# Four half tiles each on GpSimd, an adding DMA and a casting DMA: another way to split gate weights in a hybrid trunk layer

## The chip, the cores and the metric

The kernel runs on one core of one Trainium2 chip. The metric is the device time of one execution in microseconds, from runs without a profile. Beside it stands one profiled execution, whose span runs from its first to its last instruction.

## What is computed

One layer of a decoder trunk, for 256 positions of width 2048 in fp32. Cut to what matters here:

```python
h = rms_norm(x, pre_g)
a_u, a_v, a_g, b_x, b_g, x_q, x_g, gate_logits = split(h @ w_in)
y_a = spatial_gating(a_u, a_v, ...) * silu(a_g)
y_b = s5_branch(b_x, ...) * silu(b_g)
y_x = memory_cross_attention(x_q, rms_norm(mem, mem_g), wk, wv) * silu(x_g)
branch = einsum('bsnc,ncd->bsnd', stack([y_a, y_b, y_x]), w_branch)
gates = sigmoid(gate_logits)                  # 3 branches x 2048 columns
merged = sum(gates * branch, over the branches)
out = x + rms_norm(merged @ w_out, post_g)
```

The change touches the weights of `gate_logits` for one of the three branches, the cross-attention (n = 2): a matrix of 2048 x 2048.

## The kernel before, in words

**Splitting.** TensorE multiplies in the float32r format, which keeps fewer bits than fp32. So every fp32 operand is split in two: a high part, which is the operand rounded to float32r, and a low part, the operand minus the high part, rounded too. A product is made of three matmuls: high by high, high by low and low by high (`tm_mm`, L180 to L182). The split of weights stands in `split_to`: ScalarE copies the raw tile into the high part (L92), VectorE subtracts (L93).

**Tiles of weights.** `load` (L78, on SP's queue) brings a raw tile of 128 x 2048 fp32 (1 MB) from HBM; there are three such buffers (`rawp`). Each raw tile is split in two halves of 1024 columns, the half tiles. A half tile's high and low part lie in one tile called `hl`, of which there are four (`hip`, `bufs=4`). `split` makes one and marks the two instructions as early ones: `tc.high_priority(offset=AHEAD)`, with `AHEAD = 250`, moves them 250 places forward in the order in which the planner takes up instructions.

**Order.** TensorE's instructions are issued in the order in which the program writes them (`manual_schedule`). The order on the other engines is made by a planner that lays out the instructions by priority and by estimated durations when the program is built. Each engine then works through its own list in order and waits where an input isn't there or a buffer isn't free.

**Token-major products.** `tm_quarter` (L218 to L225) takes one raw tile: for each of its halves it calls `split`, then issues twelve matmuls of 512 columns (two blocks of 128 rows of weights, two blocks of 128 positions, three matmuls each), then calls `pump`. `merge(n, ...)` (L771 to L784) runs over four column blocks c of 512 columns. For each it makes the gate logits from four raw tiles (eight half tiles), takes the sigmoid (L781), makes the branch's own product from two raw tiles (four half tiles) and hands both to a sink, which multiplies them on VectorE (L791).

**Background work.** The S5 branch runs as a generator beside all this. `pump` lets it go on by a credit after each half tile; `rate["tm"]` sets the credit, and for n = 2 it is 0.33 higher in the first column block and 0.13 higher in the second. Its work is mostly VectorE's (products L371, scans L599, L374 for updates), with some on ScalarE (L530, L534, L535, L540, L548, L555) and a few matmuls (L560, L624). GpSimd issues its loads, one of 128 KB for each of 32 steps (L518, tile `sb`), and hardly anything else: one masking instruction (L814) after this merge.

**Where the merges stand.** `merge(2, ...)` is the first of the merges. In the profiled execution its column blocks c = 1, 2 and 3 run on TensorE from 265.27, 298.22 and 330.95 us of the span.

Of the kernel before, what the change touches and what calls it, by code (L numbers as in the profile page):

```python
# [9 lines left out]
F32 = mybir.dt.float32  # L10
# [3 lines left out]
AF = mybir.ActivationFunctionType  # L14
ALU = mybir.AluOpType
# [28 lines left out]
def trunk(ctx: ExitStack, tc: tile.TileContext, I, out):  # L44
    nc = tc.nc
    v, a, g, pe = nc.vector, nc.scalar, nc.gpsimd, nc.tensor
# [18 lines left out]
    def nm(s):  # L65
        n_[0] += 1
        return f"{s}_{n_[0]}"

    def slot(tag, shape, dt=F32):
        return big.tile(shape, dt, tag=tag, name=nm(tag))  # L70
# [5 lines left out]
    def load(src):  # L76
        t = rawp.tile([P, 2048], F32, tag="raw", name=nm("raw"))
        nc.sync.dma_start(out=t, in_=src)  # L78
        return t

    def halves(off):
        t = hip.tile([P, 2 * 1024 + 128], F32R, tag="hl", name=nm("hl"))
        return t[:, off:off + 1024], t[:, off + 1024:off + 2048]

    def split(src, off=0):
        hi, lo = halves(off)
        with tc.high_priority(offset=AHEAD):
            split_to(hi, lo, src)
        return hi, lo

    def split_to(hi, lo, src):
        a.copy(out=hi, in_=src)  # L92
        v.tensor_tensor(out=lo, in0=src, in1=hi.bitcast(F32), op=ALU.subtract)  # L93
# [16 lines left out]
    def acc_tile():  # L110
        return accp.tile([P, 2, 512], F32, tag="acc", name=nm("acc"))
# [67 lines left out]
    def tm_mm(ps, wh, wl, hl, tb, first, last):  # L179
        pe.matmul(ps, lhsT=hl.stationary(0, tb), rhs=two(wh), start=first, stop=False)  # L180
        pe.matmul(ps, lhsT=hl.stationary(0, tb), rhs=two(wl), start=False, stop=False)  # L181
        pe.matmul(ps, lhsT=hl.stationary(1, tb), rhs=two(wh), start=False, stop=last)  # L182
# [3 lines left out]
    def pump(credit):  # L186
        with tc.high_priority(offset=-BEHIND):
            pump_(credit)
# [21 lines left out]
    def cm_block(ps, raw, hl, mm_=cm_mm):  # L210
        for hf in range(2):
            wh, wl = split(raw[:, hf * 1024:(hf + 1) * 1024], CM_OFF)
            for k in range(8):
                kk = hf * 8 + k
                mm_(ps, wh[:, k * P:(k + 1) * P], wl[:, k * P:(k + 1) * P], hl[kk], kk == 0, kk == 15)
            pump(rate["cm"])

    def tm_quarter(acc, raw, hl, kq, nk):  # L218
        for hf in range(2):
            wh, wl = split(raw[:, hf * 1024:(hf + 1) * 1024])  # L220
            for k in range(2):
                kk = kq * 4 + hf * 2 + k
                sl = slice(k * 512, (k + 1) * 512)
                for tb in range(2):
                    tm_mm(acc[tb], wh[:, sl], wl[:, sl], hl[kk], tb, kk == 0, kk == nk - 1)  # L225
            pump(rate["tm"])
# [20 lines left out]
    xhl = [Pairs(xp.tile([P, 2, 2, P], F32R, name=f"x{k}")) for k in range(16)]  # L247
    u = slot("U", [P, 8, T])
    acc0 = [acc_tile(), acc_tile()]
    for pc in range(8):  # L250
        if pc == 0:
            raw = first
        elif pc < 3:
            raw = rawp.tile([P, 2, 768], F32, tag="raw", name=nm("st"), padded_shape=[P, 2, 1024])
        else:
            raw = slot(("H0", "H1", "H2", "H3", "M0")[pc - 3], [P, 2, 1024])[:, :, 0:768]
        wh, wl = (z.rearrange("p (q n) -> p q n", q=2) for z in halves(CM_OFF))
# [421 lines left out]
    def tm_rows(src, hl, dst, key):  # L679
        for n in range(2):  # L680
            acc = acc_tile()
            for kq in range(4):
                tm_quarter([acc[:, 0], acc[:, 1]], load(src[n, kq]), hl, kq, 16)
            for tb in range(2):
                a.activation(out=dst[:, tb, n * 512:(n + 1) * 512], in_=acc[:, tb], func=AF.Copy,
                             scale=nrm[key][0][:, tb:tb + 1])
# [84 lines left out]
    def merge(n, yhl, sink):  # L771
        for c in range(4):
            rate["tm"] = RT[6] + (0.33, 0.13, 0.0, 0.0)[c] * (n == 2)
            G = acc_tile()
            for kq in range(4):
                tm_quarter([G[:, 0], G[:, 1]], load(I["w_gate"][n, c, kq]), xhl, kq, 16)
            assert not bg[2]
            Bp = acc_tile()
            sg = wk.tile([P, 2, 512], F32, tag="w0", name=nm("g"))
            for tb in range(2):  # L780
                a.activation(out=sg[:, tb], in_=G[:, tb], func=AF.Sigmoid, scale=rstd_x[:, tb:tb + 1])  # L781
            for kq in range(2):
                tm_quarter([Bp[:, 0], Bp[:, 1]], load(I["w_br"][n, c, kq]), yhl, kq, 8)
            sink(c, sg, Bp)  # L784
# [20 lines left out]

    mg = Lazy()
    merge(2, hls(yX), sink_first)

    vt = slot("H0", [P, 2, W])
# [73 lines left out]

    cm_pairs(I["w_au"], 8, xhl, evac_au)
    merge(0, hls(yA), sink_mid)
    nrm["A"] = True

# [4 lines left out]
    for c in range(4):  # L892
        G = acc_tile()
# [10 lines left out]
    for bp in range(4):  # L904
        ps = acc_tile()
        raw = load(I["glu"][bp])
        for b in range(2):
            wh, wl = split(raw[:, b * 1024:(b + 1) * 1024], CM_OFF)
            for k in range(8):
                cm_mm(ps[:, b], wh[:, k * P:(k + 1) * P], wl[:, k * P:(k + 1) * P], ygl[k], k == 0, k == 7)  # L910
        t = fold(ps, None)
        for i in range(2):
            a.activation(out=t[:, i, :], in_=t[:, i, :], func=AF.Sigmoid, bias=glu_b[:, 2 * bp + i:2 * bp + i + 1])
        b = slice(2 * bp, 2 * bp + 2)
        v.tensor_tensor(out=t, in0=t, in1=u[:, b, :], op=ALU.mult)
        v.tensor_tensor(out=t, in0=t, in1=sb[:, b, :], op=ALU.mult)
        for i in range(2):
            d = yB[2 * bp + i]
            split_to(d[:, 0], d[:, 1], t[:, i])
# [51 lines left out]
    for n in range(3):  # L971
        acc = acc_tile()
        for kq in range(4):
            tm_quarter([acc[:, 0], acc[:, 1]], load(I["w_out"][n, kq]), mhl2, kq, 16)
            if (n * 4 + kq) in (1, 4, 7):
                dst, src = late.pop(0)
# [7 lines left out]
    acc = acc_tile()  # L984
    for kh in range(2):
        raw = load(I["w_out3"][0, kh])
        for hf in range(2):
            wh, wl = split(raw[:, hf * 1024:(hf + 1) * 1024])
# [12 lines left out]
    for kh in range(2):  # L1001
        raw = load(I["w_out3"][1, kh])
        for hf in range(2):
            src = raw[:, hf * 1024:(hf + 1) * 1024]
            if kh == 0 and hf == 0:
                for i in range(2):
                    wh = s5p.tile([P, 512], F32R, tag="s", name=nm("wh"), bufs=4)
                    wl = s5p.tile([P, 512], F32R, tag="s", name=nm("wl"), bufs=4)
                    split_to(wh, wl, src[:, i * 512:(i + 1) * 512])
                    wks += [(wh[:, k * T:(k + 1) * T], wl[:, k * T:(k + 1) * T]) for k in range(2)]  # L1010
            else:
                wh, wl = split(src)
# [5 lines left out]
    for tb in range(2):  # L1018
# [3 lines left out]
        c = slice(tb, tb + 1)  # L1022
# [107 lines left out]
```

## Time and profile before

| | |
|---|---|
| time, median of two runs | 917.31 us (917.14 to 917.48) |
| profiled execution: span | 915.4 us |
| TensorE (PE) busy | 902.2 us, 99% |
| VectorE (DVE) busy | 779.5 us, 85% |
| ScalarE (ACT) busy | 535.0 us, 58% |
| GpSimd (POOL) busy | 22.2 us, 2% |
| HBM read | 190.39 MB, 210 GB/s over the span |

The time before is that of runs without a profile; the page names the span of the profiled execution and no other time of it.

How to read the lines: a line such as `L93 DVE TENSOR_TENSOR hl<-raw,hl 128x1024 ... x319 | 388.5, 1221 | 97.3 <-ACT hl L92 93.8` is a group: line of the program, engine, operation, output and inputs, shape, count; then busy time in us and mean ns of one; then the engine's idle time just before these instructions, and what ended most of it. In order of time, a line has the start and the duration in us, and in brackets the idle time ahead of it and what released it. PEld is the weight load of a matmul, which overlaps the matmuls. A matmul's duration is modelled and longer than the distance to the next one, so TensorE's progress is read from starts. POOLq, SPq and ACTq are the queues on which DMAs are issued.

### The profile page before, as it was taken

Reading aid. Unit: us, or ns where it says so; the run is one execution under the profiler, and the core shown is the slowest. Engines: PE = TensorE matmul, PEld = TensorE weight load, DVE = VectorE, ACT = ScalarE, POOL = GpSimd, SP = SyncE. Lnnn points to the kernel's source line nnn. Section 1 sums busy time; section 2 is a strip of 40 time slices with the busy share of each in tenths; the row PEclk is TensorE's granted clock in tenths of the full one; section 3 lists DMA queues with packets and bytes.
Section 4 is the critical chain, followed back from the end, with each engine's and each line's share of the span. In section 5 each row is a group of like instructions: output and inputs, shape, how many; then the busy total and the mean of one; then the engine's idle time right before and its main releaser. Section 6 shows DMA issues by size and latency. Waiting matters only on the chain. (4 is left out here: it accounts for less than half of the span.)

```text
span 915.4 us, 12965 instructions
## 1 busy us (share of the span) xinstructions
PE 902.2 (99%) x4864; PEld 797.8 (87%) x4864; DVE 779.5 (85%) x1329; ACT 535.0 (58%) x866; POOL 22.2 (2%) x46
## 2 busy tenths in 40 slices
PE   8999999999999999999999999999999999999996
PEld 6999898899888888888899888888988888998896
DVE  7899957986789999999877999999998977876554
ACT  7576655665456576565545656756655646544452
POOL 1000000000000000000000000000000000000000
PEclk9999999999999999999999999999999999999999
DMA  9888655556355556555655555555665456657542
GB/s 343 325 304 301 218 214 194 190 192 228 138 190 193 197 197 241 214 184 200 247 184 184 190 185 193 203 193 198 227 216 213 174 208 228 218 185 276 192 176 92
DMA packets 30175, 193.33 MB, mean 211 GB/s; under 512 B 3744, under 2 KB 4128, under 8 KB 8352
## 3 DMA queue, kind: packets, MB, share of 16 engines
q1 hardware_dynamic: 28000, 186.08, 56.9%
q0 software_dynamic: 1536, 4.20, 1.4%
q10 hardware_dynamic: 576, 2.23, 0.6%
q8 instruction: 38, 0.62, 0.3%
q14 instruction: 25, 0.20, 0.1%
HBM read 190.39 MB, written 2.10 MB: 210 GB/s over the span
## 5 line engine op out<-in xcount | busy, mean ns | idle before, releaser
L93 DVE TENSOR_TENSOR hl<-raw,hl 128x1024 fp32r<-128x1024 f32 x319 | 388.5, 1221 | 97.3 <-ACT hl L92 93.8
L92 ACT CAST hl<-raw 128x1024 fp32r<-128x1024 f32 x319 | 330.2, 1045 | 182.5 <-PE acc L182 109.8
L175 PE MATMUL acc<-x,hl 128*128 128x512 f32 x736 | 241.1, 382 | 0.2 <-DVE x L169 0.2
L174 PE MATMUL acc<-x,hl 128*128 128x256 f32 x690 | 189.7, 275 | 2.1 <-DVE hl L93 1.8
L181 PE MATMUL acc<-hl,x 128*128 128x512 f32 x448 | 170.4, 380 | 1.1 <-DVE hl L93 1.0
L180 PE MATMUL acc<-hl,x 128*128 128x512 f32 x448 | 171.3, 382 | 0.0
L182 PE MATMUL acc<-hl,x 128*128 128x512 f32 x448 | 169.8, 379 | 0.0
L175 PEld LDWEIGHTS acc<-x,hl 128*128 128x128 f32 x736 | 136.7, 189 | 17.5 <-ACT hl L92 0.7
L174 PEld LDWEIGHTS acc<-x,hl 128*128 128x128 f32 x690 | 132.3, 192 | 4.9 <-DVE hl L93 3.6
L181 PEld LDWEIGHTS acc<-hl,x 128*128 128x128 f32 x448 | 84.7, 189 | 14.2 <-DVE hl L93 3.0
L180 PEld LDWEIGHTS acc<-hl,x 128*128 128x128 f32 x448 | 84.7, 189 | 13.8 <-issue 2.5
L182 PEld LDWEIGHTS acc<-hl,x 128*128 128x128 f32 x448 | 84.7, 189 | 11.8
L180 PE MATMUL acc<-hl,H 128*128 128x512 f32 (+1 forms) x224 | 83.6, 373 | 0.0
L181 PE MATMUL acc<-hl,H 128*128 128x512 f32 (+1 forms) x224 | 83.2, 372 | 0.0
L182 PE MATMUL acc<-hl,H 128*128 128x512 f32 (+1 forms) x224 | 83.2, 372 | 0.0
L175 PE MATMUL acc<-H,hl 128*128 128x512 f32 x192 | 62.8, 383 | 0.1
L174 PE MATMUL acc<-H,hl 128*128 128x256 f32 x176 | 48.3, 275 | 0.4 <-ACT H L92 0.4
L180 PEld LDWEIGHTS acc<-hl,H 128*128 128x128 f32 x224 | 42.4, 189 | 5.6 <-issue 0.4
L182 PEld LDWEIGHTS acc<-hl,H 128*128 128x128 f32 x224 | 42.4, 189 | 5.6
L181 PEld LDWEIGHTS acc<-hl,H 128*128 128x128 f32 x224 | 42.4, 189 | 5.3
L371 DVE TENSOR_TENSOR p<-p,E 128x512 f32<-128x512 f32 x64 | 44.1, 689 | 1.0
L599 DVE TENSOR_TENSOR_SCAN p<-s5r,p 128x256 f32<-128x256 f32 x64 | 42.5, 683 | 0.9
(248 smaller groups left out, 1166.4 us busy)
## 6 DMA issues: line engine op xcount, KB each, us to landing
raw<-w_gate SPq DMA_DIRECT2D x48, 1024.0 KB, 4.7
raw<-w_br SPq DMA_DIRECT2D x24, 1024.0 KB, 4.7
raw<-w_out SPq DMA_DIRECT2D x16, 1024.0 KB, 4.8
raw<-w_xq SPq DMA_DIRECT2D x8, 1024.0 KB, 5.0
raw<-wk SPq DMA_DIRECT2D x8, 1024.0 KB, 4.7
raw<-wv SPq DMA_DIRECT2D x8, 1024.0 KB, 4.8
raw<-w_xg SPq DMA_DIRECT2D x8, 1024.0 KB, 4.7
raw<-w_av SPq DMA_DIRECT2D x8, 1024.0 KB, 4.8
```

The source lines that it names most:

```text
L92: a.copy(out=hi, in_=src)
L93: v.tensor_tensor(out=lo, in0=src, in1=hi.bitcast(F32), op=ALU.subtract)
L174: pe.matmul(ps[:, 0:T], lhsT=wl, rhs=hl.moving(0), start=False, stop=False)
L175: pe.matmul(ps, lhsT=wh, rhs=hl.moving_both(), start=first, stop=last)
L180: pe.matmul(ps, lhsT=hl.stationary(0, tb), rhs=two(wh), start=first, stop=False)
L181: pe.matmul(ps, lhsT=hl.stationary(0, tb), rhs=two(wl), start=False, stop=False)
L182: pe.matmul(ps, lhsT=hl.stationary(1, tb), rhs=two(wh), start=False, stop=last)
L371: v.tensor_tensor(out=o, in0=i0, in1=i1, op=op)
L599: v.tensor_tensor_scan(out=p2[:, ri], data0=rb, data1=p1[:, ri], initial=0.0, op0=ALU.mult, op1=ALU.add)
```

## The change

In `merge`, for n = 2 alone, the second half of each gate raw tile is split in another way: in c = 1 by `"pool"`, in c = 2 by `"add"`, in c = 3 by `"cast"`. c = 0, all first halves, the branch weights and all other products keep the old way. Four raw tiles to a column block make four half tiles of each kind, twelve in all.

- `"pool"`: ScalarE makes the high part as before; GpSimd subtracts instead of VectorE.
- `"add"`: ScalarE writes the negated operand into the low part (so it is rounded there) and then the high part; a DMA on GpSimd's queue adds the raw half tile onto the low part.
- `"cast"`: a DMA on GpSimd's queue reads the half tile once more from HBM and writes it as float32r into the high part; VectorE subtracts as before.

```diff
-    def split(src, off=0):
+    def split(src, off=0, how="v", dram=None):
         hi, lo = halves(off)
         with tc.high_priority(offset=AHEAD):
-            split_to(hi, lo, src)
+            if how == "v":
+                split_to(hi, lo, src)
+            elif how == "pool":
+                a.copy(out=hi, in_=src)
+                g.tensor_tensor(out=lo, in0=src, in1=hi.bitcast(F32), op=ALU.subtract)
+            elif how == "add":
+                a.activation(out=lo, in_=src, func=AF.Copy, scale=-1.0)
+                a.copy(out=hi, in_=src)
+                g.dma_start(out=lo.bitcast(F32), in_=src, accum_op=ALU.add)
+            else:
+                g.dma_start(out=hi, in_=dram)
+                v.tensor_tensor(out=lo, in0=src, in1=hi.bitcast(F32), op=ALU.subtract)
         return hi, lo
...
-    def tm_quarter(acc, raw, hl, kq, nk):
+    def tm_quarter(acc, raw, hl, kq, nk, how="v", dram=None):
         for hf in range(2):
-            wh, wl = split(raw[:, hf * 1024:(hf + 1) * 1024])
+            sl = slice(hf * 1024, (hf + 1) * 1024)
+            wh, wl = split(raw[:, sl], 0, how if hf else "v", dram[:, sl] if dram is not None else None)
...
             for kq in range(4):
-                tm_quarter([G[:, 0], G[:, 1]], load(I["w_gate"][n, c, kq]), xhl, kq, 16)
+                src = I["w_gate"][n, c, kq]
+                how = ("v", "pool", "add", "cast")[c] if n == 2 else "v"
+                tm_quarter([G[:, 0], G[:, 1]], load(src), xhl, kq, 16, how, src)
```

## The prediction, made before the changed kernel was run

> **What bounds the kernel now.** I read the busy table first, then the costliest groups.
>
> ```profile
> span 915.4 us, 12965 instructions
> PE 902.2 (99%) x4864; PEld 797.8 (87%) x4864; DVE 779.5 (85%) x1329; ACT 535.0 (58%) x866; POOL 22.2 (2%) x46
> ...
> L93 DVE TENSOR_TENSOR hl<-raw,hl 128x1024 fp32r<-128x1024 f32 x319 | 388.5, 1221 | 97.3 <-ACT hl L92 93.8
> L92 ACT CAST hl<-raw 128x1024 fp32r<-128x1024 f32 x319 | 330.2, 1045 | 182.5 <-PE acc L182 109.8
> ```
>
> TensorE sets the end: it is busy 99% of the span, and the change takes no matmul away. Whatever relief VectorE gets, the kernel can become shorter only by TensorE waits that vanish. So the question is whether one of the twelve new splits comes later than TensorE needs it. The runs' median, 917.31 us, is 1.9 us above this span of 915.4 us; I sum on the span and add 1.9.
>
> Next, busy time in three stretches, one for each changed column block c = 1, 2, 3 of the first merge (its eight gate half tiles, then four of the branch weights).
>
> ```profile
> core 0: us, PE busy (x) PEld busy (x) DVE busy (x) ACT busy (x) POOL busy (x), PEclk, DMA share, GB/s
> 265.27:298.22 32.95, 32.95 (x168) 28.23 (x166) 31.82 (x58) 21.00 (x40) 1.08 (x2) 1.00 0.55 194
> 298.22:330.95 32.73, 32.73 (x166) 28.00 (x165) 31.72 (x54) 22.61 (x40) 1.08 (x2) 1.00 0.56 203
> 330.95:363.70 32.75, 32.75 (x156) 28.78 (x155) 31.60 (x55) 19.91 (x37) 1.61 (x3) 1.00 0.60 214
> ```
>
> TensorE is solidly busy, but VectorE too is at 97%: here it is no cover, and what is added to it comes out of its lead. ScalarE (61 to 69%) and GpSimd (3 to 5%) have room. The lead is read from the instructions in order of time: the end of a subtraction (VectorE, L93) against the first weight load of its half tile (L180).
>
> ```profile
> 259.12 1.22 DVE L93 TENSOR_TENSOR hl<-raw,hl 128x1024 fp32r<-128x1024 f32 x1
> 260.09 0.19 PEld L180 LDWEIGHTS acc<-hl,H 128*128 128x128 f32 x1
> 262.68 0.19 PEld L180 LDWEIGHTS acc<-hl,H 128*128 128x128 f32 x1
> 263.10 1.05 ACT L92 CAST hl<-raw 128x1024 fp32r<-128x1024 f32 x1 [1.54 <-PE acc L182]
> 265.27 0.19 PEld L180 LDWEIGHTS acc<-hl,x 128*128 128x128 f32 x1
> 294.70 1.22 DVE L93 TENSOR_TENSOR hl<-raw,hl 128x1024 fp32r<-128x1024 f32 x1
> 298.22 0.19 PEld L180 LDWEIGHTS acc<-hl,x 128*128 128x128 f32 x1
> 314.54 1.20 DVE L93 TENSOR_TENSOR hl<-raw,hl 128x1024 fp32r<-128x1024 f32 x1
> 316.57 0.19 PEld L180 LDWEIGHTS acc<-hl,x 128*128 128x128 f32 x1
> 346.81 1.22 DVE L93 TENSOR_TENSOR hl<-raw,hl 128x1024 fp32r<-128x1024 f32 x1
> 349.62 0.19 PEld L180 LDWEIGHTS acc<-hl,x 128*128 128x128 f32 x1
> ```
>
> A half tile lasts 2.59 us on TensorE (260.09 to 262.68). The split of a half tile can start when TensorE has left the buffer of four half tiles earlier: the cast at 263.10 begins 0.42 us after the boundary at 262.68. From there it has three half tiles, 7.77 us. Today's lead is 4.9 us as c = 1 begins (260.34 to 265.27), 2.3 us at its end (295.92 to 298.22), 0.8 us in the last gate half tile of c = 2 (315.74 to 316.57), 1.6 us in the last of c = 3 (348.03 to 349.62). Thin, but nowhere late.
>
> **c = 1: four subtractions on GpSimd.** VectorE loses 4 x 1.22 = 4.9 us of work, ScalarE keeps its cast, GpSimd gets four two-input subtractions. The trace has none. Its nearest row is a one-input instruction of the same size, and it shows something else:
>
> ```profile
> 365.27 1.09 POOL L814 TENSOR_SCALAR_AFFINE_SELECT H<-H 128x1024 f32<-128x1024 f32 x1 [7.47 <-DMA H<-sg_wT]
> ...
> 342.26 0.76 DVE L371 TENSOR_TENSOR p<-p,p 128x256 f32<-128x256 f32 x2
> ...
> 365.36 1.61 DVE L371 TENSOR_TENSOR p<-p,p 128x256 f32<-128x256 f32 x2
> ...
> 368.87 0.19 PEld L181 LDWEIGHTS acc<-hl,x 128*128 128x128 f32 x1 [0.81 <-DVE hl L93]
> ```
>
> The VectorE pair that started beside GpSimd's 1.09 us took 1.61 us where the same form took 0.76: 0.85 us longer, 78% of GpSimd's time. And TensorE waited 0.81 us for a VectorE subtraction soon after, one of its few waits. So a GpSimd subtraction is not free for VectorE. Its own price I bound by 1.1 us (one input as dear as two) and 4.4; I take 2.2, the row once per input, as the row's work is one pass over one input. VectorE is held 0.78 x 2.2 = 1.7 us for each 1.22 it is spared, 4 x 0.5 = 1.9 us more work. The lead of 2.3 us at the end of c = 1 covers that: **0 us**. Without that lead it would cost the 1.9. At 1.1 us VectorE gains 1.5 us, worth nothing to TensorE; at 4.4 it loses 4 x (3.4 - 1.22) = 8.7 us, less the 2.3 of lead and the 0.9 that it idles (next fence): 5.5 us late. The half tile's own path is short: 0.4 + 1.05 for the cast, one VectorE instruction of up to 1.2 ahead, 2.2: 4.9 of 7.77 us.
>
> The Trainium skill (SBUF — State Buffer, Who interferes with whom) says that a VectorE instruction with two SBUF inputs and a GpSimd instruction that reads SBUF exclude each other for the whole instruction. The stretched pair agrees, 0.85 of 1.09 us. Taken as the whole 2.2 us, VectorE's extra would be 4 x 0.96 = 3.8 us and, less 2.3 and 0.9, 0.6 us late: the sum would be 0.6 us higher.
>
> **c = 2: four subtractions by an adding DMA.** VectorE loses another 4.9 us, ScalarE gets four more copies (4.2 us, in its idle 10 us), and GpSimd issues four DMAs of 512 KB that read the raw half tile and the negated high part and write the low part. No row shows an adding DMA; the transfers and waits of this stretch (281 to 331 us; VectorE's waits 265 to 331 us) are these:
>
> ```profile
> q1 hardware_dynamic: 1296, 9.44, 52.3%
> ...
> raw<-w_gate SPq DMA_DIRECT2D x8, 1024.0 KB, 4.8
> ...
> sb<-s5b POOLq DMA_DIRECT2D x3, 128.0 KB, 3.7
> ```
>
> ```profile
> DVE gl L368 <- ACT gl L643: 0.6, 2, 0.3
> DVE s L371 <- PE y L624: 0.3, 1, 0.3
> ```
>
> A megabyte occupies the 16 engines 0.523 x 50 / 9.44 = 2.8 us of its 4.8; 2.0 are latency. By bytes written the add is half a raw load, 2.0 + 1.4 = 3.4 us; by bytes read it is a whole one, 4.8. Today a raw load is in flight most of the time (4.8 of every 5.2 us), and GpSimd's 128 KB took 3.7 us beside it, where engine time says 2.4. I take a whole load plus half of another's engine time: 4.8 + 1.4 = 6.2 us; bounds 3.4 and 9.4 (twice 4.8). From the free buffer: 1.0 until ScalarE starts (0.4 and its S5 work ahead), 2.1 for two ScalarE passes, 0.1 to GpSimd, 6.2: 9.4 us against 7.77, 1.6 late. The late half tiles are every second one: of four, the second and the fourth got their buffers before the delay struck, so it is paid twice: **3.3 us**. At 3.4 us it is 0, at 9.4 us 2 x 4.8 = 9.7 us. VectorE's relief here finds no buyer: its lead is capped by the four buffers. The raw tile is freed some 2 us later; two more raw tiles cover that.
>
> **c = 3: four high parts by a casting DMA.** ScalarE loses four casts; a DMA of 512 KB from HBM takes their place; VectorE keeps its subtraction but waits for that DMA. It can be issued when the buffer is free, 0.5 us after; 3.4 us at the least, 3.4 + 1.4 = 4.8 to 6.2 us beside a raw load. At 5.2 us the high part is there 5.7 us after the buffer; with 1.2 for the subtraction it is 6.9 of 7.77, so the half tile itself is in time. But VectorE works in order, and behind a waiting subtraction stand the S5 instructions and the next subtractions. Today's subtractions start 3.0, 3.8, 3.8 and 5.3 us after the buffer is free (the last at 346.81, freed at 341.53):
>
> ```profile
> 325.77 0.19 PEld L180 LDWEIGHTS acc<-hl,H 128*128 128x128 f32 x1
> 328.80 1.23 DVE L93 TENSOR_TENSOR hl<-raw,hl 128x1024 fp32r<-128x1024 f32 x1
> 330.95 0.19 PEld L180 LDWEIGHTS acc<-hl,x 128*128 128x128 f32 x1
> 334.74 1.23 DVE L93 TENSOR_TENSOR hl<-raw,hl 128x1024 fp32r<-128x1024 f32 x1
> 336.45 0.19 PEld L180 LDWEIGHTS acc<-hl,x 128*128 128x128 f32 x1
> 340.21 1.22 DVE L93 TENSOR_TENSOR hl<-raw,hl 128x1024 fp32r<-128x1024 f32 x1
> 341.53 0.19 PEld L180 LDWEIGHTS acc<-hl,x 128*128 128x128 f32 x1
> ```
>
> Kept at those places VectorE would stand 2.7 + 1.9 + 1.9 + 0.4 = 6.9 us. The order is made anew, with S5 work moved ahead of a subtraction whose input is late, so it is less; between 0 and 6.9 I take 2.0. The lead is 1.6 us here and gone at 368.87, so all of it reaches TensorE: **2.0 us**.
>
> On GpSimd's queue each new instruction stands among the S5 loads. The one issued at 261.42 feeds a cast at 274.03, 12.6 us later, so a few us of waiting ahead of it stay hidden:
>
> ```profile
> 261.42 0.54 POOL L518 DMA_DIRECT2D sb<-s5b  x1 [64.07 <-DVE B L531]
> 274.03 0.39 ACT L530 CAST B<-sb 128x256 fp32r<-128x256 f32 x1
> 279.35 0.54 POOL L518 DMA_DIRECT2D sb<-s5b  x1 [17.40 <-ACT hl L92]
> ```
>
> The sum: 915.4 + 0 + 3.3 + 2.0 = 920.7, and with 1.9: **922.6 us**. Since TensorE never idles afterwards, nothing of it is caught up.
>
> **The rivals.** *Everything hidden (not slower).* If the adding DMA lands within 4.6 us (7.77 - 3.2) and the casting one is ordered well, no half tile is late; the 0.8 us wait at 368.87 may vanish with VectorE's spared work. For it: lead everywhere, transfers use 55 to 60% of the DMA time. Against: the loads already fill that time in bursts. About 917.0 us.
>
> *GpSimd is the slow one.* At 4.4 us a subtraction, or with GpSimd itself held back by VectorE's 97%, c = 1 alone adds 5.5: 928 us. It decides where a subtraction passes 2.6 us (0.78 x 2.6 - 1.22 = 0.81; four times that is the 3.2 us of lead and idle). For it: the stretched pair. Against: nothing shows a second input costing more than the first.
>
> *The adding DMA is slow.* If it moves like eight separate 128 KB reads of 3.7 - 2.0 = 1.7 us each, it lands after 15.6 us: 1.0 + 2.1 + 0.1 + 15.6 = 18.8, twice 11.0 late, 22 us: 941 us. Slower by over 2% begins near 14 us. Against: the 4.2 MB of GpSimd's queue show nothing of the kind. The Trainium skill (Collectives: The Full Stack, Part 3) says that a reducing transfer is bound by its two reads, not by the add; no run here shows it.
>
> *The order on GpSimd fails (the change does not do what it says).* If a new instruction stands behind an S5 load that waits, as the one at 279.35 did 17.4 us long, its half tile is late: a subtraction started at 279.9 for use at 279.6 ends 2.5 us late. About 925 us.
>
> **How the numbers follow.** The forecast 0.45, hidden 0.27, GpSimd slow 0.12, DMA slow 0.11, order 0.05. The range runs from 916.6 (hidden, with a little of the vanished wait) to 935 us (the forecast with two costs at their upper bounds, 6.4 more for the adding DMA and 5.5 for GpSimd, 934.5); outside are most of the slow DMA and a sliver below. A measurement can tell about 2% (18 us) from no change: faster by more than that has no mechanism (0.01), the slow DMA is slower (0.11), all else within (0.88).
>
> **What would show it.** Right: TensorE waits in c = 2 released by the adding DMA, 1 to 2 us in two or more half tiles; VectorE waits for DMAs in c = 3; VectorE instructions stretched beside GpSimd in c = 1 without a TensorE wait. Wrong: an adding DMA under 4.6 us or over 9.4, GpSimd subtractions over 2.6 us, or TensorE waits outside these three blocks, by instructions reordered elsewhere.

## The result, and the profile after

The changed kernel takes 924.65 us (two runs, 923.67 and 925.64), against 917.31 us before: a ratio of 1.008 with an interval of 1.005 to 1.0109, so 7.3 us slower. The prediction said 922.6 us within 916.6 to 935. The profiled execution has a span of 923.9 us, 8.5 more than before. The first lines are from the page of the changed kernel: span, busy times and the two groups of the split.

```profile
span 923.9 us, 13001 instructions
...
PE 904.1 (98%) x4864; PEld 800.3 (87%) x4864; DVE 777.7 (84%) x1321; ACT 534.8 (58%) x866; POOL 37.9 (4%) x58
...
L104 DVE TENSOR_TENSOR hl<-raw,hl 128x1024 fp32r<-128x1024 f32 x307 | 374.0, 1221 | 104.2 <-ACT hl L103 101.7
L103 ACT CAST hl<-raw 128x1024 fp32r<-128x1024 f32 x307 | 318.1, 1044 | 190.5 <-PE acc L193 116.8
```

The group of VectorE's subtractions has 307 instead of 319; four of the twelve stand behind the casting DMA on a line of their own (L99), so eight are gone, 8 x 1.22 = 9.8 us. Yet VectorE's busy time falls by only 1.8 us, from 779.5 to 777.7: its other work became 8.0 us dearer. TensorE's number of matmuls is the same. Next, the same three stretches as before, from the start of one gate product to the next (c = 1, 2, 3; the columns as in the prediction's fence).

```profile
266.06:300.25 34.19, 33.42 (x167) 28.13 (x166) 31.22 (x49) 19.28 (x38) 8.22 (x5) 1.00 0.51 172
300.25:341.38 41.13, 35.09 (x165) 29.02 (x164) 31.51 (x59) 27.84 (x48) 5.78 (x8) 0.96 0.79 245
341.38:374.14 32.76, 32.76 (x156) 28.85 (x155) 32.46 (x55) 17.59 (x34) 2.96 (x6) 1.00 0.79 277
```

The three blocks lasted 32.95, 32.73 and 32.75 us before; now they last 34.19, 41.13 and 32.76. So c = 1 costs 1.24 us, c = 2 costs 8.40, and c = 3 nothing. The mean granted clock of c = 2 is 0.96 where it was 1.00. Two smaller differences lie outside. The changed kernel is 0.79 us late already as c = 1 begins (266.06 against 265.27), from the very first loads, which the change does not touch; the other kernels below, whose start is the same, lie between 0.29 us early and 1.04 us late there, so this is chance. And after c = 3 it wins 1.86 us back: its lag behind the kernel before is 10.44 us at 374 us, 9.76 as the next product begins (416.44 against 406.68), and 8.58 from 504 us to the end. Together 0.79 + 1.24 + 8.40 - 1.86 = 8.57.

TensorE's long waits stand in its weight loads, in order of time, with the idle time and its releaser in brackets:

```profile
289.86 0.19 PEld L192 LDWEIGHTS acc<-hl,H 128*128 128x128 f32 x1 [1.07 <-DVE hl L104]
...
306.70 0.19 PEld L192 LDWEIGHTS acc<-hl,x 128*128 128x128 f32 x1 [3.18 <-DMA hl<-raw]
...
315.42 0.29 PEld L192 LDWEIGHTS acc<-hl,x 128*128 128x128 f32 x1 [3.34 <-DMA hl<-raw]
```

The first is the branch product of c = 1, waiting for a VectorE subtraction. The other two are half tiles of c = 2, waiting for the adding DMA. Before's wait of 0.8 us at 368.87 is gone.

### The profile page after: what moved, and what is told of

The parts are those of the page before. It is cut to its first block, busy times and chain, and to the rows that moved or that the text cites. A ratio compares the mean times of both kernels' runs of the same rounds, so it can differ in the third digit from the quotient of the medians.

```text
span 923.9 us, 13001 instructions
## 1 busy us (share of the span) xinstructions
PE 904.1 (98%) x4864; PEld 800.3 (87%) x4864; DVE 777.7 (84%) x1321; ACT 534.8 (58%) x866; POOL 37.9 (4%) x58
## 5 line engine op out<-in xcount | busy, mean ns | idle before, releaser
L104 DVE TENSOR_TENSOR hl<-raw,hl 128x1024 fp32r<-128x1024 f32 x307 | 374.0, 1221 | 104.2 <-ACT hl L103 101.7
L103 ACT CAST hl<-raw 128x1024 fp32r<-128x1024 f32 x307 | 318.1, 1044 | 190.5 <-PE acc L193 116.8
L611 DVE TENSOR_TENSOR_SCAN p<-s5r,p 128x256 f32<-128x256 f32 x64 | 46.7, 750 | 0.9
```

Source lines behind the costliest of these rows:

```text
L611: v.tensor_tensor_scan(out=p2[:, ri], data0=rb, data1=p1[:, ri], initial=0.0, op0=ALU.mult, op1=ALU.add)
```

## The experiments

In the diffs, the line with `how` is that of `merge` in the changed kernel. Times are medians; each ratio is against the kernel before, run on the same chip.

**One part at a time.**

```diff
-                how = ("v", "pool", "add", "cast")[c] if n == 2 else "v"
+                how = ("v", "pool", "v", "v")[c] if n == 2 else "v"    # GpSimd subtractions alone
+                how = ("v", "v", "add", "v")[c] if n == 2 else "v"     # adding DMAs alone
+                how = ("v", "v", "v", "cast")[c] if n == 2 else "v"    # casting DMAs alone
```

> Only the four GpSimd subtractions of c = 1; c = 2 and c = 3 as before. My theory (VectorE is held during each GpSimd subtraction of 2.37 us, so it does 4 x (2.1 - 1.22) = 3.7 us more, and no adding DMA relieves it in c = 2): the lead of 0.8 us at the end of c = 2's gate runs out as well, TensorE waits about 2 us in all on VectorE subtractions, 919 us. Rival (GpSimd's cost is only what the changed kernel shows inside c = 1): 1.2 us, 918.5 us. Rival (the large loss in c = 2 is a late effect of c = 1, through ScalarE waiting on a late VectorE): then this kernel alone costs 4 us or more, over 921 us.

> Only the four adding DMAs of c = 2. Theory A (the add's own path is too long: two ScalarE passes in a list that S5 work shares, then 4.6 to 7.8 us of transfer): TensorE waits for the DMA in two half tiles, 6 to 8 us lost there, some of it given back later, 922 to 924 us. Theory B (ScalarE reached the adds late only because GpSimd had held VectorE back in c = 1): ScalarE starts the first add within 3 us of the free buffer instead of 5.6, the loss is 3 us or less, under 920.5 us.

> Only the four casting DMAs of c = 3. Theory (the cast path is in time: landing 3.5 to 4.4 us, three half tiles of cover): no wait in c = 3, 917.3 us within 0.5. Rival 1 (in the changed kernel VectorE had caught up during TensorE's waits in c = 2, and this hid the casts' cost): VectorE waits for the DMA and TensorE loses about 2 us, 919 us. Rival 2 (the 1.9 us that the changed kernel gains back after the merge come from the casts): faster, 915.5 us.

Measured: GpSimd alone 921.69 us, 1.0049 (1.0036 to 1.0062), 4.2 us slower. Adding DMAs alone 923.41 us, 1.0069 (1.0055 to 1.0083), 6.0 us slower. Casting DMAs alone 916.30 us, 0.9986 (0.9977 to 0.9995), 1.2 us faster, which beats both kernels. So all three prices were missed: GpSimd is not free, the add costs nearly twice the forecast, and the cast is a small gain. Of the expectations, the second rival's time held for GpSimd (4 us or more), theory A's for the adds, and none quite for the casts, which came out between the theory and the second rival. The views show how.

GpSimd alone. First GpSimd's own rows, then VectorE's at the same times, then the same two VectorE instructions in the kernel before:

```profile
273.78 2.37 POOL L92 TENSOR_TENSOR hl<-raw,hl 128x1024 fp32r<-128x1024 f32 x1 [3.78 <-ACT hl L91]
...
280.24 2.36 POOL L92 TENSOR_TENSOR hl<-raw,hl 128x1024 fp32r<-128x1024 f32 x1 [0.26 <-ACT hl L91]
```

```profile
274.06 2.47 DVE L383 TENSOR_TENSOR U<-U,gl 128x256 f32<-128x256 f32 x1 [0.34 <-ACT gl L659]
...
280.30 3.44 DVE L611 TENSOR_TENSOR_SCAN p<-s5r,p 128x256 f32<-128x256 f32 x2
...
287.62 1.23 DVE L104 TENSOR_TENSOR hl<-raw,hl 128x1024 fp32r<-128x1024 f32 x1 [0.51 <-ACT hl L103]
```

```profile
274.35 0.50 DVE L371 TENSOR_TENSOR U<-U,gl 128x256 f32<-128x256 f32 x1
...
278.84 1.28 DVE L599 TENSOR_TENSOR_SCAN p<-s5r,p 128x256 f32<-128x256 f32 x2
```

The subtraction takes 2.37 us. The product at 274.06 ends 0.38 us after GpSimd's instruction, and took 2.47 us; the scans at 280.30 end 1.14 us after it and took 3.44, where the same pair took 1.28 us before. Over the four subtractions VectorE was held about 2.1 + 0.75 + 2.0 + 2.2 = 7.0 us, for 4.9 us that it was spared. That is what the prediction had (6.8 for 4.9). What it did not have follows in ScalarE's rows and TensorE's:

```profile
283.94 0.51 ACT L567 ACTIVATE E<-E 128x128 f32<-128x128 f32 x2 [3.79 <-DVE E L386]
...
286.56 1.03 ACT L103 CAST hl<-raw 128x1024 fp32r<-128x1024 f32 x1
```

```profile
288.90 0.19 PEld L192 LDWEIGHTS acc<-hl,H 128*128 128x128 f32 x1 [1.07 <-DVE hl L104]
...
373.11 0.19 PEld L192 LDWEIGHTS acc<-hl,x 128*128 128x128 f32 x1 [1.81 <-DVE hl L104]
```

ScalarE works in order and stands 3.79 us for VectorE's update of E; behind it stands the cast of the next half tile, which now starts at 286.56 instead of 284.12. VectorE then waits 0.51 us for that cast (287.62), and TensorE 1.07 us for VectorE. In 260 to 372 us VectorE's waits for high parts grow from the first of these lines (before) to the second (GpSimd alone). The third is the kernel in which GpSimd only fills (below):

```profile
DVE hl L93 <- ACT hl L92: 0.5, 1, 0.5
```

```profile
DVE hl L104 <- ACT hl L103: 2.1, 3, 1.1
```

```profile
DVE hl L105 <- ACT hl L104: 2.1, 3, 1.1
```

It looks as if the hold came round to VectorE through ScalarE, but the fills hold VectorE nowhere, and the same three waits stand there (0.51 us at 283.21, 1.12 at 285.94, 0.45 at 351.99). They come with the new order of the lists, in which the subtraction is gone from VectorE's list and S5 work stands elsewhere. VectorE's waits in all grow from 1.9 to 4.0 us there. The sizes fit: 2.1 us of extra work by the hold and 2.1 of extra waiting by the order are the 4.2 us. They are not paid in c = 1 alone: against the kernel before, TensorE loses 1.2 us in c = 1, 2.0 in c = 2, in steps of about half a microsecond, and 1.2 from the end of c = 3 on, where the old wait of 0.8 us at 368.87 is now one of 1.8 (373.11).

Adding DMAs alone. ScalarE's rows, GpSimd's issue, the landing times (least, median, most) and TensorE's waits:

```profile
294.96 0.24 ACT L552 COPY E<-ebase 128x64 f32<-128x64 f32 x1 [1.67 <-DVE p L383]
295.24 0.35 ACT L560 ACTIVATE t<-E,pwr 128x64 f32<-128x64 f32 x1
295.50 1.05 ACT L94 ACTIVATE hl<-raw 128x1024 fp32r<-128x1024 f32 x1
296.45 1.03 ACT L95 CAST hl<-raw 128x1024 fp32r<-128x1024 f32 x1
```

```profile
296.85 0.90 POOL L96 DMA_DIRECT2D hl<-raw  x1 [4.98 <-ACT hl L94]
```

```profile
DMA to landing us min/median/max: 5.7/6.4/7.9
```

```profile
PE acc L192 <- DMA hl<-raw: 3.8, 3, 1.7
```

The buffer of this half tile was free at about 293.0 us (two half tiles after TensorE passed to the branch product). The negating pass began 2.5 us later, not 1.0: ahead of it on ScalarE stand two S5 instructions, and the first waits 1.67 us for a VectorE product. The DMA was issued 1.35 us after the pass began, before the second pass had ended, so one ScalarE pass counts and not two. Then 6.3 us to the landing: 2.5 + 1.35 + 6.3 = 10.2 of the 7.8 us there are. Three of the four adds made TensorE wait. The profiled execution is the fastest of this kernel's five, 921.21 us; it lost 4.6 us in c = 2, and what the others lost beyond that was not seen.

Casting DMAs alone. GpSimd's issue and VectorE's subtraction of the first of them:

```profile
326.62 0.54 POOL L98 DMA_DIRECT2D hl<-w_gate  x1 [11.72 <-DVE hl L104]
```

```profile
331.82 1.22 DVE L99 TENSOR_TENSOR hl<-raw,hl 128x1024 fp32r<-128x1024 f32 x1
```

The subtraction starts 5.2 us after the issue and has no wait in its brackets: S5 work was put ahead of it, and the DMA had landed. The term of 2.0 us does not exist here. VectorE waits for no DMA in this block, and TensorE's 0.8 us wait of before at 368.87 us is gone. That part of the gain is not the cast's own: in the same product TensorE wins back 0.67 us in the kernel with the adding DMAs alone and in that without their DMA, and 0.42 with the fills.

**What the adding DMA's price is made of.**

```diff
-                g.dma_start(out=lo.bitcast(F32), in_=src, accum_op=ALU.add)
+                g.dma_start(out=lo.bitcast(F32), in_=src)      # plain DMA
+                                                               # no DMA at all
-                a.activation(out=lo, in_=src, func=AF.Copy, scale=-1.0)
-                g.dma_start(out=lo.bitcast(F32), in_=src, accum_op=ALU.add)
+                a.activation(out=lo[:, 0:512], in_=src[:, 0:512], func=AF.Copy, scale=-1.0)
+                g.dma_start(out=lo[:, 0:512].bitcast(F32), in_=src[:, 0:512], accum_op=ALU.add)
+                v.tensor_tensor(out=lo[:, 512:1024], ...)      # half by DMA, half on VectorE
```

(All three in the kernel with the adding DMAs alone.)

> As the kernel with the adding DMAs alone, but the DMA copies the raw half tile over the low part instead of adding to it (the subtraction is left out, so the low part is not the low part). Orders and issues are the same; only the transfer reads once instead of twice. If the double reading makes the add late: engine time falls from 2.7 to 1.4 us, landing to 3.5 to 5.5 us, and TensorE's waits in c = 2 shrink by 1.3 to 2.5 us for each late half tile, 3 us or more in all. If the late start on ScalarE is the cause and the transfer is not: within 1 us of the kernel with the adding DMAs.

> As the kernel with the adding DMAs alone, without the DMA: ScalarE still makes two passes for each of the four half tiles, the subtraction is left out (the low part stays the negated operand). Theory (the transfer is what is late, and VectorE's spared 4.9 us are worth at most the few waits that TensorE has afterwards): no wait in c = 2, 916 to 917 us. Rival (ScalarE's second pass in a list shared with S5 work is already too late): TensorE waits for ScalarE in c = 2, 918.5 us or more.

> Adding DMAs in c = 2 alone, each for 512 of the 1024 columns (256 KB); VectorE subtracts the other 512. If the transfer's size makes the add late: half the engine time, 1.35 us, landing 3.5 to 5.5 us instead of 5.7 to 7.9, in time or nearly: 917 to 918.5 us. If it is the latency and the sharing of the queues, whatever the size: 920 us or more.

Measured: plain DMA 919.19 us, 1.0024 (1.0014 to 1.0033), 1.7 us slower than before; no DMA 916.96 us, 0.9996 (0.9987 to 1.0005), no difference; half 918.34 us, 1.0011 (1.0002 to 1.0019), 1.0 us slower. So the four extra ScalarE passes and VectorE's relief together are worth nothing; all 6.0 us hang on the transfer, by the medians 1.7 on any transfer at this place and 4.3 on its being an add. The profiles show less of that difference: in c = 2 TensorE lost 3.4 us with the plain DMA, in the slowest of ten runs, and 4.6 with the add, in the fastest of five. The add's runs spread over 3.9 us; whether a slow clock after a long stop (last section) is part of that was not seen. The plain DMA's issue, its landing times, and the half add's landing times:

```profile
297.50 0.53 POOL L96 DMA_DIRECT2D hl<-raw  x1 [4.97 <-ACT hl L94]
```

```profile
DMA to landing us min/median/max: 3.3/5.8/7.1
```

```profile
DMA to landing us min/median/max: 5.0/5.8/6.8
```

The plain one costs GpSimd 0.53 us to issue against 0.90, and lands 0.6 us sooner by the median (5.8 against 6.4); in order of issue the first two, for both of which TensorE waits, land after 5.0 and 6.6 us against 6.3 and 7.9. Half the bytes land 0.6 us sooner than the whole add by the median, the first two after 5.3 and 6.8 us, so most of the 6 us does not go by bytes; the prediction had 2.0 us of latency and 4.2 in proportion to the bytes. The half add also has half a negating pass ahead of it and is issued 0.6 us sooner (the first at 296.29 against 296.85 us). Together that leaves one TensorE stop over 1 us where there were two of 2.

**What holds VectorE beside GpSimd.**

```diff
-                g.tensor_tensor(out=lo, in0=src, in1=hi.bitcast(F32), op=ALU.subtract)
+                for _ in range(2): g.memset(lo.bitcast(F32), 0.0)    # writes alone
+                g.tensor_copy(out=lo, in_=src)                       # one input
```

(Each in the kernel with the GpSimd subtractions alone.)

> As the kernel with the GpSimd subtractions alone, but GpSimd fills the low part with zeros twice (some 1.8 us of work that reads nothing) instead of subtracting; the low part of four half tiles is left out. Theory (what holds VectorE is GpSimd's reading): no VectorE instruction is stretched beside the fills, VectorE has 4.9 us less to do, 916 to 917 us. Rival (any GpSimd instruction of that length holds VectorE): scans stretched by some 1.6 us each time, 4 x (1.6 - 1.22) = 1.5 us more on VectorE, 919 us.

> As the kernel with the GpSimd subtractions alone, but GpSimd copies the raw half tile (one input) instead of subtracting; the subtraction is left out. Theory (a GpSimd instruction takes about 1.1 to 1.2 us for each input and holds VectorE for as long): 1.1 to 1.2 us each, VectorE stretched by 0.9 to 1.1 us, about what it is spared, 916.5 to 918 us. Rival (the price is the instruction's and not the input's): about 2.3 us each and a loss near that of the subtractions, 920 us or more.

Measured: fills 916.93 us, 0.9997 (0.9988 to 1.0006), nothing lost; copies 918.86 us, 1.0015 (1.0006 to 1.0023), 1.5 us lost; subtractions 4.2. GpSimd's and VectorE's rows, the fills first and then the copies:

```profile
272.17 1.96 POOL L93 MEMSET hl<- 128x1024 f32 x2 [4.48 <-ACT t L561]
```

```profile
272.40 0.49 DVE L384 TENSOR_TENSOR gl<-gl,U 128x256 f32<-128x256 f32 x1
...
273.56 0.52 DVE L384 TENSOR_TENSOR U<-U,gl 128x256 f32<-128x256 f32 x1 [0.47 <-ACT gl L660]
```

```profile
272.84 1.10 POOL L92 CAST hl<-raw 128x1024 fp32r<-128x1024 f32 x1 [5.14 <-PE bu L572]
```

```profile
272.97 1.36 DVE L383 TENSOR_TENSOR gl<-gl,U 128x256 f32<-128x256 f32 x1
```

Beside 1.96 us of fills the two-input products keep their 0.49 and 0.52 us. Beside a copy of 1.10 us the first of them takes 1.36, 0.87 more. Beside the subtraction the second took 2.47 (above), 1.95 more. So the hold is some 80 to 90% of the GpSimd instruction's time when that instruction reads and the two overlap from its start, and none when it only writes; the second input doubles the instruction and with it the hold. The Trainium skill (SBUF — State Buffer, Who interferes with whom) says just that: a VectorE instruction with two SBUF inputs contends with a GpSimd instruction that reads SBUF, not with one that only writes. The runs agree, 0.87 and 1.95 us against none. GpSimd is held as well: the two of its four copies that were issued while VectorE subtracted took 1.39 and 1.44 us, the other two 1.04 and 1.10.

The loss does not follow the hold alone. Beside the four copies VectorE was held 2.4 us in all for the 4.9 that it was spared, and yet 1.5 us were lost, between the two expectations. The rest is waiting: VectorE's waits from 260 to 372 us are 1.9 us before, 6.1 with the fills, 5.4 with the copies and 4.0 with the subtractions. Hold less 4.9 us of spared work, plus the waits added, is 0 - 4.9 + 4.2 = -0.7 us for the fills, 2.4 - 4.9 + 3.5 = 1.0 for the copies and 7.0 - 4.9 + 2.1 = 4.2 for the subtractions. From the start of c = 1 to 407 us TensorE gains 0.4, loses 1.3 and loses 4.4.

**Where a cast is free.**

```diff
-                how = ("v", "pool", "add", "cast")[c] if n == 2 else "v"
+                how = ("v", "cast", "cast", "cast")[c] if n == 2 else "v"   # three blocks
+                how = "cast" if c == 3 else "v"                             # last block of two merges
```

> The casting DMA in c = 1, 2 and 3 (twelve casts, no GpSimd subtraction, no adding DMA). Theory (the cast is in time, and it spares ScalarE 1.05 us each, which lets S5 work and splits start earlier): no wait in the three blocks, 915 to 916.5 us, as good as the casts in c = 3 alone or better. Rival (where the lead is 0.8 us, in c = 2, VectorE stands waiting for the DMA): TensorE waits on a VectorE subtraction there, 918 us or more.

> The casting DMA in the last column block (c = 3) of the first and of the second merge, nothing else changed. The kernel before has waits of TensorE on a VectorE subtraction near the end of both. Theory (a cast spares ScalarE and lets VectorE's waits for it vanish, where S5 work can be moved ahead of the subtraction): the wait of 0.75 us near the end of the second merge goes as well, 915.5 us. Rival (it is luck of the order in the first merge): as the casts in the first merge alone, 916.3 us, or slower by VectorE standing for a DMA in the second, 917.5 us or more.

Measured: three blocks 921.47 us, 1.0046 (1.0033 to 1.0058), 4.1 us slower; the last blocks of two merges 918.78 us, 1.0017 (1.0008 to 1.0026), 1.5 us slower, where the first merge's alone was 1.2 faster. In both the rival's time held, though not the way it was to come about: the cast isn't free by itself, but at that one place. For three blocks, a VectorE row of c = 1:

```profile
273.14 1.23 DVE L99 TENSOR_TENSOR hl<-raw,hl 128x1024 fp32r<-128x1024 f32 x1 [5.04 <-DMA hl<-w_gate]
```

This is the stall that the prediction feared for c = 3: VectorE stands 5 us for a casting DMA, which landed 7.5 us after its issue, and everything queued behind it is late. In c = 2 VectorE waits for no DMA, yet TensorE waits 0.6 to 1.2 us for each of the four subtractions behind a cast. For the second merge, the landing time of one cast (issued at 587.99 us), the VectorE rows up to its subtraction, and TensorE's wait:

```profile
DMA to landing us min/median/max: 5.0/5.0/5.0
```

```profile
592.95 0.42 DVE L543 TENSOR_TENSOR B<-sb,B 64x256 fp32r<-64x256 f32 x1
593.41 1.27 DVE L611 TENSOR_TENSOR_SCAN p<-s5r,p 128x256 f32<-128x256 f32 x2
594.72 1.42 DVE L383 TENSOR_TENSOR p<-p,E 128x512 f32<-128x512 f32 x2
596.17 0.76 DVE L383 TENSOR_TENSOR s<-p,p 128x256 f32<-128x256 f32 x2
596.85 1.22 DVE L99 TENSOR_TENSOR hl<-raw,hl 128x1024 fp32r<-128x1024 f32 x1
```

```profile
598.12 0.19 PEld L192 LDWEIGHTS acc<-hl,x 128*128 128x128 f32 x1 [2.85 <-DVE hl L99]
```

The high part was there at 593.0 us. The subtraction started at 596.85, because 3.9 us of S5 work had been put ahead of it when the order was made; TensorE needed it at 595.3 and waited 2.85 us. So the same reordering that hides the DMA in the first merge is too much in the second. No DMA is late here; the subtraction's place in VectorE's list is.

**Do the two losses add?** GpSimd subtractions and adding DMAs without the casts:

```diff
+                how = ("v", "pool", "add", "v")[c] if n == 2 else "v"
```

> GpSimd subtractions in c = 1 and adding DMAs in c = 2, no casts. Alone they cost 4.2 and 6.0 us. If the two losses are separate, they add: 927.6 us. If TensorE's waits for the DMA in c = 2 give VectorE the time to catch up on what GpSimd cost it, part is paid only once: the changed kernel's 924.65 and the 1.2 us that the casts alone gain, 925.8 us or less.

Measured: 926.71 us, 1.0100 (1.0084 to 1.0115), 9.4 us slower; alone they were 4.2 and 6.0, 10.2 together. Nearly additive, and between what the two theories expected, so neither is shown. The profile of this kernel holds a loss of 1.7 us by a slow clock (last section) that the profiles of the two parts do not have. The whole change, with the casts, is at 924.65 us, 2.1 less.

## Why the prediction was right, and where its steps were wrong

The total was right, 5.3 us forecast and 7.3 found, and so was the class of the answer: TensorE sets the end, VectorE's relief found no buyer, the adding DMA makes TensorE wait. But the three terms of the sum were 0, 3.3 and 2.0 us, and alone they measure 4.2, 6.0 and -1.2: two too small and one too large, and they cancelled in part. That the total came so near is luck.

**c = 1, forecast 0.** The work was sized rightly: 2.37 us for a subtraction (2.2 forecast), VectorE held 7.0 us for 4.9 spared. (Where the working takes the whole 2.2 us as the hold, 2.2 - 1.22 is 0.98 and not 0.96, which makes its 0.6 us 0.7.) The step that failed is "the lead of 2.3 us at the end of c = 1 covers that". It looked at one place and at VectorE alone. The lead is shorter at other places (0.8 us in c = 2, none at 368.87), VectorE at 97% never earns it back before them, and the new order of the lists, a term that the sum put at nothing, brought another 2.1 us of VectorE waits. The fills show that these are not GpSimd's doing: they have the same waits for high parts and lose nothing, as VectorE has 4.9 us less to do.

**c = 2, forecast 3.3.** The transfer was forecast at 6.2 us and took 5.7 to 7.9 (alone; 4.6 to 7.8 in the changed kernel). Two ScalarE passes were charged and one counts. The start on ScalarE was forecast 1.0 us after the buffer is free and came 2.5 and 3.0 us after for the first two, behind S5 instructions that wait for VectorE. And with the adding DMAs alone the wait struck three half tiles, not two, the first two of them one after the other; in the changed kernel it struck two. There, c = 2 inherits c = 1's lateness:

```profile
299.91 0.24 ACT L552 COPY E<-ebase 128x64 f32<-128x64 f32 x1 [2.84 <-DVE p L383]
300.19 0.35 ACT L560 ACTIVATE t<-E,pwr 128x64 f32<-128x64 f32 x1
300.44 1.04 ACT L94 ACTIVATE hl<-raw 128x1024 fp32r<-128x1024 f32 x1
```

ScalarE stands 2.84 us for the VectorE product instead of 1.67. That longer wait is the new order's: with the fills alone it is 2.84 us too, and the pass after it begins at 295.08. What is late is the product, behind VectorE's held work: the pass begins 4.9 us later than with the adding DMAs alone (295.50), while TensorE is only 1.9 us later. So the waits grow from 2.0 and 2.1 us to 3.2 and 3.4. Of the changed kernel's 8.40 us in c = 2, then, a part is c = 1's price, and some 1.6 us are the clock's (last section).

**c = 3, forecast 2.0.** In this place the reorder was enough: the step that failed is that VectorE would stand 2.0 us for the DMA, and it stood for none. The forecast's doubt (VectorE in order behind a waiting subtraction) was a real mechanism, shown by the other two placements, but not here.

**"Since TensorE never idles afterwards nothing is caught up"** is wrong: 1.86 us came back between 374 and 504 us, where the kernel before had waits of 0.8 us and less. In the kernel with the casts alone, TensorE gains 0.67 and 0.39 us on the kernel before in the same two products. The kernel with GpSimd subtractions and adding DMAs, which has the same long stops and no casts, wins back 0.66 us in the first product and none in the second. So 0.7 us come back without the casts, and 1.2 only with them; why the casts bring more here than alone was not tried.

Of the signs named in advance: the GpSimd rows stayed under 2.6 us, and yet the subtractions alone cost 4.2, so that bound was the wrong sign; no VectorE wait for a DMA in c = 3; TensorE waits released by the adding DMA in two half tiles, yes, but 3 us long.

## What to carry to other kernels

Where the engine that is spared work is itself at 97%, add up its work and its waits, in the new order of the lists, up to the place where the lead is smallest; a lead at one place says little. Leaving an instruction out of one list changes the waits of the others, as the fills show. A transfer that replaces an instruction of 1.2 us must be set against its whole latency, here 3.3 to 7.9 us, from a point as early as the buffer is free; where the issuing chain itself stands behind other work, it is late. And where the order is fixed at build time, the same edit can be free in one place and bring a wait of 2.85 us in the next: price it for each place.

## What the runs showed of the chip

**The clock after a wait.** The 41.13 us of c = 2 hold more than the waits. The changed kernel's windows from 304 to 319.4 us (columns as before; the granted clock is the third figure from the end):

```profile
304.00:312.00 8.00, 5.29 (x26) 4.69 (x26) 7.87 (x13) 6.36 (x12) 1.46 (x2) 1.00 0.76 199
312.00:315.40 3.40, 0.38 (x3) 0.08 (x1) 3.20 (x8) 3.33 (x7) 0.87 (x1) 0.97 1.06 229
...
316.00:319.00 3.00, 3.00 (x9) 2.43 (x8) 2.87 (x6) 0.00 (x0) 0.57 (x1) 0.57 0.95 309
319.00:319.20 0.20, 0.20 (x2) 0.17 (x2) 0.20 (x1) 0.00 (x0) 0.00 (x0) 1.00 1.16 492
```

After the 3.34 us wait that ended at 315.42 the clock is half until about 318.6 us, and TensorE loses some 1.6 us more; after the wait of 3.18 us that ended at 306.70 it stays at 1.00. In the kernel with GpSimd subtractions and adding DMAs, a wait of 2.47 us (ended 314.78) was enough:

```profile
304.00:312.00 8.00, 5.23 (x24) 4.46 (x24) 7.87 (x14) 6.37 (x12) 1.47 (x2) 1.00 0.78 202
...
315.80:319.40 3.60, 3.60 (x11) 2.86 (x10) 3.47 (x7) 0.72 (x2) 0.57 (x1) 0.53 1.00 307
```

The Trainium skill (TensorE: Matmul & The Clock Gate, Part 1) says that the clock falls to half after an idle window of about 3.4 us and comes back after one of about 3.4 us of activity, and that the windows run freely and do not start anew with the kernel. The length of the slow stretch agrees (about 3.4 us both times). That a wait of 3.18 us passes and one of 2.47 does not fits windows that run freely: in the changed kernel the clock falls at about 315.2 us (0.97 over the second row), and counted back from there in steps of 3.4 us a window ends at 305.0, which cuts the 3.18 us in two parts of about 1.4 and 1.7. But 2.47 us is no whole idle window, so here less than a fully idle one was enough. Free-running windows would also let the same kernel differ between runs: with the casts in two merges, the runs with a mean clock of 0.997 took 917.3 to 918.0 us and those with 0.995 took 919.3 to 920.4. That this is the wait of 2.85 us at 598 us, slow in some runs and not in others, is argued and not shown.

**An adding DMA** of 512 KB within the chip occupies GpSimd 0.88 us at issue, a plain one 0.53. By the median it lands after 5.2 us in the changed kernel, 5.8 with GpSimd subtractions and adding DMAs, and 6.4 with the adding DMAs alone; with 256 KB it is 5.8. So the kernels differ more than the two sizes do.
